# Six of eight output tiles of a 512-token projection as seven-product pairs on one Trainium2 core

## The chip, the cores and the metric

The kernel runs on one core of one Trainium2 chip, in one launch. The metric is the device time of that core in microseconds (us): the median of three runs of the kernel before is 1076.18 us (1074.87 to 1076.5). Differences of a few us, that is of a few tenths of a per cent, are what this case is about. Every number with a row shown beside it comes from one profiled execution, whose instructions are stamped in us from the start of its span.

## The reference, cut to what matters

One decoder layer is applied to 512 prompt tokens and 64 sample tokens (T = 576 columns together). Its first block, the mixer, runs two kinds of heads and joins them by one projection; two further blocks (cross attention to a memory of 256 rows, and a gated feed-forward net) follow.

```python
proj = u @ w_in                                   # u: (tokens, 1024)
...
y_ssd = _rms(...) * g_ssm_out                     # first half of the mixer's output, 1024 wide
h_ml = _rms(h_ml).reshape(bsz, length, ML_INNER) * g_mlstm_out * jax.nn.sigmoid(og)   # second half, 1024 wide
mix = jnp.concatenate([y_ssd, h_ml], axis=-1) @ w_out     # (tokens, 2048) @ (2048, 1024)
x = x + _rms(mix) * g_post_mix
```

The change concerns `y_ssd @ w_out[0:1024]`, the first half of that last product: 1024 x 1024 weights by 1024 x 576 activations.

## The kernel before, in words

**Layout and precision.** Activations lie with features on the 128 partitions and tokens along the free axis, as `[128, 8, 576]` (eight k-tiles of 128 features). Each float32 operand is split into a high part (a rounding cast by ScalarE, `A.copy` into an fp32r tile) and a low part (the rest, subtracted by VectorE); a product is three matmuls per k-tile: high by high, high by low, low by high. An output tile of 128 features thus takes 2 token parts x 8 k-tiles x 3 = 48 matmuls, with the token parts `HALVES` = 256 and 320 columns wide.

**Weights.** `split_w` loads 512 KB into `raw` (two buffers, from the SP queue), casts into `whi` (three buffers, ScalarE, L191) and makes `wlo` (three buffers, VectorE, L198). Where VectorE is spared, the low part is made by a transfer instead: ScalarE writes minus the high part, and a DMA on the POOL queue adds the raw weights from HBM to it.

**The stretch around the change.** The last tiles of the input projection (`in_tile(29 + j, ...)`, "og" tiles; their evacuations are L1133, L1134, L1136) end together with the last mLSTM head, whose normalisation runs on VectorE and GpSimd (`head_norm`, L941 to L954, then L1000) and whose result TensorE transposes (L1004, `ht`, then copied to `qk` at L1005). Between them `gn_apply` (L1122) scales `y` and splits it into `mixs_h` and `mixs_l`. Then come eight calls `out1(j)`: the first half of the output projection, 16 token parts evacuated to `f` by ScalarE (L1154). The first may not go ahead of `ht` on TensorE (`issue_after`). Early in this stretch `mixm_h` and `mixm_l`, the split second half of the mixer's output, are made from `qk` (L1160, L1161), and the samples' part of it from `ogs` (L1165, L1166). Then follow the calls `out2(j, i)`: the second half, added to `f` by VectorE (L1288), with squares and a scaled copy by ScalarE.

**Work placed beside it.** `presplit` takes eight weight matrices of later stages (list `PRE`): load to `prel` (POOL queue), cast (L1244, ScalarE), low part (L1245, VectorE), store to HBM (POOL queue); their casts stand between 403.9 and 442.0 us. `memraw` (the memory, in the slot that held `qk`) is loaded in four pieces during `out1(4)` to `out1(7)`, split by `memory()` (L1274, L1275) and squared; `wm_split` prepares four matrices for the memory's keys and values; `x` takes over that slot afterwards (L1297, two loads) and is first used by `chain2` (L1191).

**Order.** Outside a few stretches written out by hand, a list scheduler decides the order on each engine from a model of the instructions' times: what is ready goes first by place in the program. The order is then fixed; each engine and each queue (SP, POOL) takes its instructions in that order. `tc.issue_after(i)` puts what is in its block behind instruction `i`. Memory of a closed pool is given to the next one; the first write of a new tile waits for the last reader of the old one.

**The same scheme elsewhere.** The feed-forward block already multiplies pairs of output tiles in seven products instead of eight (`Seven`, `Pair`, L1862 to L1998; a Winograd form of the 2 x 2 block product: two feature tiles by two halves of the tokens, two halves of the inner axis). Its token parts are `EHALVES`, 288 columns each, its mixed sums of the activations come from four subtractions (L1825) with casts (L1837) and low parts (L1842), and its mixed sums of the weights are L1898 to L1922.

```python
def mul(s, ps, w, b, start=True):                 # one of the seven products, L1939
    ...
    for k in range(nk):                           # 4 k-tiles
        mm(ps, wh, b[0][k], ...); mm(ps, wh, b[1][k], ...); mm(ps, wl, b[0][k], ...)
```

## Time and profile before

| | |
|---|---|
| three runs | 1074.87, 1076.18, 1076.5 us |
| the profiled execution | 1074.69 us; its span 1072.9 us; granted TensorE clock 0.999 |
| TensorE (PE) busy | 1063.1 us, 99% of the span |
| VectorE (DVE), ScalarE (ACT), GpSimd (POOL) busy | 757.7, 608.9 and 231.0 us |
| moved by DMA | 181.74 MB, 169 GB/s over the span |

How to read it: PE is TensorE's matmuls, PEld its weight loads. A busy share is a share of the time shown, and for PE it says nothing of the rate, so rates are read from the starts of successive matmuls. In a row of a timeline stand the start in us, the duration in us, the engine, the line of the kernel, the operation, output and inputs; in square brackets the idle time ahead of it and what ended it. A row of a line's or tile's listing gives the count and the shortest, median and longest duration in ns. A row of stages gives a stretch, its length, and the busy time of each engine in it (with counts).

### The profile page before, as it was taken

The numbers are of one execution on the slowest core, as the hardware profiler recorded it, in microseconds if no ns is written. First come the engines' busy times: TensorE is split into PE (matmuls) and PEld (weight loads), VectorE is DVE, ScalarE is ACT, GpSimd is POOL, SyncE is SP. The second block draws the span as 40 slices with busy tenths as digits, with TensorE's granted clock in tenths as the row PEclk, the third lists the DMA queues.
The fourth block names the chain that finished last, engine by engine and source line by source line (L and its number), as shares of the span: only waits on it lengthen the run. The fifth ranks groups of instructions, "written<-read, shape, count | busy, mean of one in ns | idle before, by whom it ended". The sixth has DMA issues, their size and how long they took to land.

```text
span 1072.9 us, 20686 instructions
## 1 busy us (share of the span) xinstructions
PE 1063.1 (99%) x8096; PEld 1011.0 (94%) x8096; DVE 757.7 (71%) x1523; ACT 608.9 (57%) x1102; POOL 231.0 (22%) x305
## 2 busy tenths in 40 slices
PE   9999999999999999999999999999999999999997
PEld 8999887778999999999999989999999999999997
DVE  6798775658878774758755556766467887787556
ACT  7778523345654555655555445645566566656654
POOL 0454543313213111000154201100011111111000
PEclk9999999999999999999999999999999999999999
DMA  6776544425655349642468775743476687578532
GB/s 209 176 162 132 158 134 172 147 89 168 196 150 152 106 143 330 235 170 98 158 213 288 265 256 176 254 124 98 133 179 137 160 188 178 114 191 188 144 119 89
DMA packets 58965, 181.74 MB, mean 169 GB/s; under 512 B 6604, under 2 KB 12108, under 8 KB 58356
## 3 DMA queue, kind: packets, MB, share of 16 engines
q1 hardware_dynamic: 42884, 138.22, 38.7%
q0 software_dynamic: 15408, 41.43, 19.7%
q8 instruction: 63, 1.03, 0.4%
q10 hardware_dynamic: 576, 0.79, 0.2%
q14 instruction: 34, 0.28, 0.1%
HBM read 159.75 MB, written 20.65 MB: 168 GB/s over the span
## 4 chain that ended last, share of the span: by engine, by line
PE 98%; DVE 0%; DMA 0%; POOL 0%; issue 0%; ACT 0%; SPq 0%; DVEq 0%
PE ps_in L215 7%; PE ps_in L218 7%; PE ps_in L216 7%; PE ps_v L882 5%; PE ps_g L1946 3%; PE ps_u L1946 3%; PE ps_g L1945 3%; PE ps_o L218 3%; PE ps_o L216 3%; PE ps_u L1947 3%; PE ps_g L1947 3%; PE ps_o L215 3%; PE ps_u L1945 3%; PE ps_dn L1945 2%; PE ps_dn L1947 2%; PE ps_dn L1946 2%
## 5 line engine op out<-in xcount | busy, mean ns | idle before, releaser
L215 PE MATMUL ps_in<-uh,whi 128*128 128x320 f32 (+1 forms) x544 | 162.6, 299 | 0.0
L218 PE MATMUL ps_in<-uh,wlo 128*128 128x320 f32 (+1 forms) x544 | 161.6, 298 | 0.0
L216 PE MATMUL ps_in<-ul,whi 128*128 128x320 f32 (+1 forms) x544 | 161.1, 296 | 0.0
L191 ACT CAST whi<-raw 128x1024 fp32r<-128x1024 f32 (+1 forms) x104 | 105.4, 1015 | 93.3 <-PE ps_in L216 21.5
L198 DVE TENSOR_TENSOR wlo<-raw,whi 128x1024 fp32r<-128x1024 f32 (+2 forms) x97 | 95.3, 983 | 63.7 <-ACT whi L191 63.0
L215 PEld LDWEIGHTS ps_in<-uh,whi 128*128 128x128 f32 x544 | 102.3, 188 | 1.9 <-issue 0.8
L218 PEld LDWEIGHTS ps_in<-uh,wlo 128*128 128x128 f32 x544 | 102.2, 188 | 1.9 <-issue 1.3
L216 PEld LDWEIGHTS ps_in<-ul,whi 128*128 128x128 f32 x544 | 102.4, 188 | 0.5
L196 POOL DMA_DIRECT2D wlo<-win x31 | 27.2, 877 | 80.2 <-ACT wlo L195 69.9
L1945 PE MATMUL ps_g<-b,whi 128*128 128x288 f32 x144 | 42.4, 295 | 0.0
L1946 PE MATMUL ps_g<-b,whi 128*128 128x288 f32 x144 | 42.3, 294 | 0.0
L1946 PE MATMUL ps_u<-b,whi 128*128 128x288 f32 x144 | 42.2, 294 | 0.0
L1945 PE MATMUL ps_u<-b,whi 128*128 128x288 f32 x144 | 42.2, 294 | 0.0
L1905 DVE TENSOR_TENSOR wlo<-sw,whi 128x1024 fp32r<-128x1024 f32 (+1 forms) x26 | 29.6, 1139 | 16.8 <-ACT whi L1904 16.8
L1918 ACT CAST whi<-rawx 128x1024 fp32r<-128x1024 f32 (+1 forms) x26 | 25.6, 986 | 26.2 <-PE ps_dn L1946 13.3
L1895 ACT CAST whi<-raw 128x1024 fp32r<-128x1024 f32 (+1 forms) x26 | 25.6, 985 | 22.8 <-PE ps_g L1946 11.8
L215 PE MATMUL ps_xo<-qh,whi 128*128 128x288 f32 x128 | 38.2, 301 | 0.0
L216 PE MATMUL ps_xo<-ql,whi 128*128 128x288 f32 x128 | 37.8, 297 | 0.0
L218 PE MATMUL ps_o<-mixm_h,wlo 128*128 128x256 f32 (+1 forms) x128 | 37.5, 293 | 0.0
L216 PE MATMUL ps_o<-mixm_l,whi 128*128 128x256 f32 (+1 forms) x128 | 37.5, 293 | 0.0
L218 PE MATMUL ps_xq<-u2h,wlo 128*128 128x320 f32 (+1 forms) x128 | 37.5, 294 | 0.0
L218 PE MATMUL ps_o<-mixs_h,wlo 128*128 128x320 f32 (+1 forms) x128 | 37.4, 293 | 0.0
(788 smaller groups left out, 3855.6 us busy)
## 6 DMA issues: line engine op xcount, KB each, us to landing
raw<-win SPq DMA_DIRECT2D x35, 512.0 KB, 4.4
raw<-wout SPq DMA_DIRECT2D x17, 512.0 KB, 4.2
raw<-wxq SPq DMA_DIRECT2D x13, 512.0 KB, 4.7
raw<-wgate SPq DMA_DIRECT2D x13, 512.0 KB, 3.3
raw<-wup SPq DMA_DIRECT2D x13, 512.0 KB, 4.7
wlo<-win POOLq DMA_DIRECT2D x24, 256.0 KB, 5.6
kva<-vc SPq DMA_DIRECT2D x11, 512.0 KB, 5.9
raw<-wv SPq DMA_DIRECT2D x10, 512.0 KB, 4.0
```

The costliest lines, as they stand in the source:

```text
L191: casts.append(A.copy(hi[:, :n], raw[:, :n]))
L196: accs.append(G.dma_start(lo[:, a:b], src[:, a:b], accum_op=ALU.add))
L198: e.tensor_tensor(lo[:, a:b], raw[:, a:b], hi[:, a:b].bitcast(F32), op=ALU.subtract)
L215: mm(ps, wh, ah, start=i == 0, stop=False)
L216: products.append(mm(ps, wh, al, start=False, stop=False))
L218: m = mm(ps, tiles[order[c]][1], xh(order[c], t0, n), start=False, stop=c == len(tiles) - 1)
L882: mm(ps, a, b, skip_group_check=True, **kw)
L1895: s.c1 = A.copy(s.h1[:, s.all], s.r1[:, s.all])
L1905: V.tensor_tensor(s.l2[:, s.all], sw[:, s.all], s.h2[:, s.all].bitcast(F32), op=ALU.subtract)
L1945: mm(ps, wh, b[0][k], start=start and k == 0, stop=False, skip_group_check=True)
L1946: mm(ps, wh, b[1][k], start=False, stop=False, skip_group_check=True)
L1947: m = mm(ps, wl, b[0][k], start=False, stop=k == nk - 1, skip_group_check=True)
```

## The change

Tiles 0 and 1 of the first half stay as they are. Tiles 2 to 7 become three pairs of a new class `Mixed`, which do what the feed-forward pairs do: seven products of four k-tiles with 288 columns, summed in two places by TensorE in one bank and otherwise by VectorE into `f` (`put`). The activations' four mixed sums are made in place in `y` (`mixed_sums`), with high and low parts in a new pool `mixsums`; the weights' sums use a new pool `mixweights` that takes the memory of the closed mLSTM pools. The first weights' low part comes from VectorE for the first pair and by transfer for the other two. One operand of each pair (`h4`, `ls`) is written over columns of `mixs_h` and `mixs_l` that are no longer read. `ghalf` is kept in place of the parameters `g_ml`; the samples' part of `mixm` is made ahead of `out1(0)`, the rest of `mixm` three, three and two tiles at a time behind each pair's last cast and last low part. One of the eight matrices made ahead (`raw_ahead`, `low_ahead`, `store_ahead`) is done during the pairs, with the low part by transfer; the other seven, and the memory's loads, move behind the pairs into the second half of the projection.

```diff
-    ghalf = ml.tile([P, KT], F32, name="ghalf")
-    V.tensor_scalar(ghalf, PAR("g_ml"), 0.5, None, op0=ALU.mult)
+    ghalf = PAR("g_ml")
+    V.tensor_scalar(ghalf, ghalf, 0.5, None, op0=ALU.mult)
...
+    sos = ExitStack()
+    wo = sos.enter_context(tc.tile_pool(name="mixsums", bufs=1, side="right", reuse_waits="tile"))
+    tmh, tml = [[wo.tile([P, 4, 288], F32R, name=k + str(m), tag=k + str(m)) for m in range(4)] for k in ("tmh", "tml")]
+    ES = [slice(t0, t0 + n) for t0, n in EHALVES]
+    (M11, M12), (M21, M22) = [[y[:, 4 * k:4 * k + 4, c] for c in ES] for k in range(2)]
...
+    def mixed_sums(*ops):
+        for m, o, p, q in ops:
+            V.tensor_tensor(o, p, q, op=ALU.subtract)
+            split(tmh[m], tml[m], o)
...
+    mixed_sums((0, M11, M12, M11), (2, M12, M22, M12), (1, M22, M22, M11), (3, M21, M21, M22))
+
+    def mixm_parts(js, p_):
+        for j in js:
+            hm = qk[:, 4 * (j % 2) + j // 2, 0:TP]
+            with tc.issue_after(p_.cast.ins):
+                A.activation(mixm_h[:, j, 0:TP], hm, AF.Copy, scale=ghalf[:, j:j + 1])
+            with tc.issue_after(p_.low.ins):
+                V.scalar_tensor_tensor(mixm_l[:, j, 0:TP], hm, ghalf[:, j:j + 1], mixm_h[:, j, 0:TP].bitcast(F32),
+                                       op0=ALU.mult, op1=ALU.subtract)
...
+    mixm_samples()
+    stv.close()
+    svs = ExitStack()
+    wv = svs.enter_context(tc.tile_pool(name="mixweights", bufs=1, reuse_waits="tile"))
...
+    HA, HB, HALL = slice(0, 512), slice(512, 1024), slice(0, 1024)
+    m11, m21, m22 = [[[t_[:, 4 * k + m, c] for m in range(4)] for t_ in (mixs_h, mixs_l)]
+                     for k, c in ((0, ES[0]), (1, ES[0]), (1, ES[1]))]
+    tm = [[[t_[m][:, k, :] for k in range(4)] for t_ in (tmh, tml)] for m in range(4)]
...
+    class Mixed:
+        def __init__(s, j):
+            s.j, s.side = j, j // 2 % 2
+            src = [I["wout"][j + k, 0] for k in range(2)]
+            s.r1 = wp.tile([P, 1024], F32, name="raw", tag="raw", bufs=2)
+            s.r2 = wv.tile([P, 1024], F32, name="rawm", tag="rawm", bufs=2)
+            for r, w in zip((s.r1, s.r2), src):
+                loads.append(S.dma_start(r, w))
+            h1, h2, h3 = [wp.tile([P, 1024], F32R, name="whi", tag="whi", bufs=3) for _ in range(3)]
+            l2, l3 = [wp.tile([P, 1024], F32R, name="wlo", tag="wlo", bufs=3) for _ in range(2)]
+            l1 = wv.tile([P, 1024], F32R, name="waccm", tag="waccm", bufs=2)
+            h4, ls = [t_[:, 0:4, 288 + P * s.side:416 + P * s.side] for t_ in (mixs_h, mixs_l)]
+            sm = wv.tile([P, 1024], F32, name="swm", tag="swm")
+            d4 = wv.tile([P, 512], F32, name="d4m", tag="d4m")
+            def low_by_transfer(out, raw, w):
+                A.activation(out, raw, AF.Copy, scale=-1.0)
+                G.dma_start(out, w, accum_op=ALU.add)
+            if j == 2:
+                with tc.issue_after(evs[1].ins):
+                    A.copy(h1, s.r1)
+                V.tensor_tensor(l1, s.r1, h1.bitcast(F32), op=ALU.subtract)
+            else:
+                low_by_transfer(l1, s.r1, src[0])
+                A.copy(h1, s.r1)
+            low_by_transfer(l3[:, HA], s.r2[:, HB], src[1][:, HB])
+            V.tensor_tensor(sm[:, HB], s.r2[:, HA], s.r2[:, HB], op=ALU.add)
+            V.tensor_tensor(sm[:, HA], sm[:, HB], s.r1[:, HA], op=ALU.subtract)
+            split(h2, l2, sm)
+            V.tensor_tensor(s.r2[:, HA], s.r1[:, HA], s.r2[:, HA], op=ALU.subtract)
+            V.tensor_tensor(d4, s.r1[:, HB], sm[:, HA], op=ALU.subtract)
+            A.copy(h3, s.r2)
+            V.tensor_tensor(ls, k4(s.r2[:, HA]), k4(h3[:, HA]).bitcast(F32), op=ALU.subtract)
+            s.cast = A.copy(h4, k4(d4))
+            s.low = V.tensor_tensor(k4(l3[:, HB]), k4(d4), h4.bitcast(F32), op=ALU.subtract)
+            s.w = [(k4(h1[:, HA]), k4(l1[:, HA])), (k4(h1[:, HB]), k4(l1[:, HB])), (k4(h2[:, HA]), k4(l2[:, HA])),
+                   (k4(h2[:, HB]), k4(l2[:, HB])), (k4(h3[:, HA]), ls), (k4(h3[:, HB]), k4(l3[:, HA])), (h4, k4(l3[:, HB]))]
+        def bank(s):
+            return (MP if s.side else GP)("ps_o")[:, :288]
+        def mul(s, ps, w, b, start=True):
+            fh, fl = s.w[w]
+            for k in range(4):
+                mm(ps, fh[:, k, :], b[0][k], start=start and k == 0, stop=False, skip_group_check=True)
+                mm(ps, fh[:, k, :], b[1][k], start=False, stop=False, skip_group_check=True)
+                m = mm(ps, fl[:, k, :], b[0][k], start=False, stop=k == 3, skip_group_check=True)
+            return m
+        def put(s, a, i, ps, first):
+            o = f[:, s.j + a, ES[i]]
+            if first:
+                evs.append(A.copy(o, ps))
+            else:
+                V.tensor_tensor(o, o, ps, op=ALU.add)
+        def early(s):
+            s.x, y_ = s.bank(), s.bank()
+            with tc.issue_after(whole.ins) if s.j == 2 else ExitStack():
+                s.mul(s.x, 0, m11)
+            s.put(0, 0, s.x, True)
+            s.mul(y_, 1, m21)
+            s.put(0, 0, y_, False)
+        def mid(s):
+            s.mul(s.x, 2, tm[1], False)
+            s.put(0, 1, s.x, True)
+            s.z = s.bank()
+            s.mul(s.z, 3, tm[0])
+            s.mul(s.x, 4, tm[2], False)
+            s.put(1, 1, s.x, True)
+            s.put(1, 1, s.z, False)
+        def late(s):
+            s.mul(s.x, 5, tm[3], False)
+            s.put(1, 0, s.x, True)
+            s.mul(s.z, 6, m22, False)
+            s.put(0, 1, s.z, False)
...
+    PRE = [("xo", 0), ("xo", 1), ("g", 0), ("u", 0), ("g", 1), ("u", 1), ("g", 2), ("u", 2)]
+    pre = dr.tile([P, len(PRE), 1024], F32, name="pre")
+    ahead, turns = [], list(range(len(PRE)))
+    def ahead_src(n):
+        k, j = PRE[n]
+        return I[{"xo": "wxo", "g": "wgate", "u": "wup"}[k]][j]
+    def raw_ahead():
+        n_ = turns.pop(0)
+        t_ = wv.tile([P, 1024], F32R, name="prem", tag="prem")
+        G.dma_start(t_, ahead_src(n_))
+        return n_, t_
+    def low_ahead(n_, t_, p_):
+        with tc.issue_after(p_.cast.ins):
+            A.activation(t_, t_.bitcast(F32), AF.Copy, scale=-1.0)
+        G.dma_start(t_, ahead_src(n_), accum_op=ALU.add)
+    def store_ahead(n_, t_, p_):
+        with tc.issue_after(p_.low.ins):
+            S.dma_start(pre[:, n_, :], t_.bitcast(F32))
+    def presplit(n, left):
+        while len(ahead) > left:
+            n_, t_ = ahead.pop(0)
+            h_ = at.tile([P, 1024], F32R, name="preh", tag="prh", bufs=1)
+            with tc.issue_after(evs[-1].ins):
+                A.copy(h_, t_)
+            V.tensor_tensor(t_, t_, h_.bitcast(F32), op=ALU.subtract)
+            G.dma_start(pre[:, n_, :], t_)
+        for _ in range(n):
+            n_ = turns.pop(0)
+            t_ = at.tile([P, 1024], F32, name="prel", tag=("pr", "prl", "mv")[n_ % 3], bufs=1)
+            G.dma_start(t_, ahead_src(n_))
+            ahead.append((n_, t_))
     def out1(j):
         with tc.issue_after(ht.ins) if j == 0 else ExitStack():
-            gemm2([(*split_w(I["wout"][j, 0], cut=1024), KT)], act(mixs_h), act(mixs_l),
-                  lambda t0, n, ps: evs.append(A.copy(f[:, j, t0:t0 + n], ps)), "ps_o1")
+            return gemm2([(*split_w(I["wout"][j, 0], cut=1024), KT)], act(mixs_h), act(mixs_l),
+                         lambda t0, n, ps: evs.append(A.copy(f[:, j, t0:t0 + n], ps)), "ps_o1")
     out1(0)
-    for j in range(8):
-        hm = qk[:, 4 * (j % 2) + j // 2, 0:TP]
-        with tc.issue_after((evs[0] if j > 2 else htc).ins):
-            A.activation(mixm_h[:, j, 0:TP], hm, AF.Copy, scale=ghalf[:, j:j + 1])
-        V.scalar_tensor_tensor(mixm_l[:, j, 0:TP], hm, ghalf[:, j:j + 1], mixm_h[:, j, 0:TP].bitcast(F32),
-                               op0=ALU.mult, op1=ALU.subtract)
-    o4 = ogs.rearrange("p (h d) t -> p h d t", d=2)
-    for d in range(2):
-        V.scalar_tensor_tensor(o4[:, :, d], o4[:, :, d], 1.0, qk[:, 4 * d:4 * d + 4, TP:T], op0=ALU.add, op1=ALU.mult)
-    V.tensor_tensor(ogs, ogs, ghalf.unsqueeze(2).to_broadcast([P, KT, TS]), op=ALU.mult)
-    split(mixm_h[:, :, TP:T], mixm_l[:, :, TP:T], ogs)
-    stv.close()
+    early_low = raw_ahead()
+    whole = out1(1)
+    before = None
+    for j in (2, 4, 6):
+        pair_ = Mixed(j)
+        pair_.early()
+        if before:
+            before.late()
+        pair_.mid()
+        before = pair_
+        if j == 4:
+            low_ahead(*early_low, pair_)
+        elif j == 6:
+            store_ahead(*early_low, pair_)
+        mixm_parts(range(*{2: (0, 3), 4: (3, 6), 6: (6, 8)}[j]), pair_)
+    before.late()
+    svs.close()
+    sos.close()
     phs = ExitStack()
...
-    for j in range(8):
-        if j:
-            out1(j)
-        presplit(min(len(turns), 1 if j else 2))
-        if j > 3:
-            k2 = slice(2 * j - 8, 2 * j - 6)
-            with tc.issue_after(loads[-1].ins):
-                S.dma_start(memraw[:, k2, :], I["memT"][:, k2, :])
+    presplit(2, 0)
+    for j in range(4):
+        k2 = slice(2 * j, 2 * j + 2)
+        with tc.issue_after(loads[-1].ins):
+            S.dma_start(memraw[:, k2, :], I["memT"][:, k2, :])
     def memory(ks):
...
     for j in range(4):
         out2(j, 1)
         out2(j, 0)
-        presplit(0, 0)
+        presplit(min(len(turns), 2 if j else 1), 1 if j < 3 else 0)
         memory(range(2 * j, 2 * j + 2))
         wm_split(j)
     memory_norm()
```

The pool `mixsums` lies on the right side of the core's memory and is closed, like `mixweights`, ahead of the pools of the next block (`rows`, `attn`), which thus take over its memory.

More of the change, by code (lines that the diff above doesn't have):

```diff
@@ new lines, in mixm_samples @@
+    def mixm_samples():
+        o4 = ogs.rearrange("p (h d) t -> p h d t", d=2)
+        for d in range(2):
+            V.scalar_tensor_tensor(o4[:, :, d], o4[:, :, d], 1.0, qk[:, 4 * d:4 * d + 4, TP:T], op0=ALU.add, op1=ALU.mult)
+        V.tensor_tensor(ogs, ogs, ghalf.unsqueeze(2).to_broadcast([P, KT, TS]), op=ALU.mult)
+        split(mixm_h[:, :, TP:T], mixm_l[:, :, TP:T], ogs)
+    mixm_samples()
+    stv.close()
+    svs = ExitStack()
+    wv = svs.enter_context(tc.tile_pool(name="mixweights", bufs=1, reuse_waits="tile"))
@@ L1147, in build, with k4 @@
     f = SL(5, "f_mix")
     evs = []
+    def k4(t_):
+        return t_.rearrange("p (k c) -> p k c", c=P)
+    HA, HB, HALL = slice(0, 512), slice(512, 1024), slice(0, 1024)
[73 more added lines that the diff above has]
+            s.put(0, 1, s.z, False)
```

18 lines of the change are left out of this document (removed).

## The prediction

> **What bounds the kernel now.** I read the page's busy shares and its chain first, then TensorE's waits.
>
> ```profile
> PE 1063.1 (99%) x8096; PEld 1011.0 (94%) x8096; DVE 757.7 (71%) x1523; ACT 608.9 (57%) x1102; POOL 231.0 (22%) x305
> ...
> PE 98%; DVE 0%; DMA 0%; POOL 0%; issue 0%; ACT 0%; SPq 0%; DVEq 0%
> ```
> ```profile
> PE ps_warm L337 <- DVE wz L334: 1.1, 1, 1.1
> PE ps_in L378 <- ACT uh L361: 1.0, 1, 1.0
> PE ps_rb L1693 <- DVE px_r L1686: 0.6, 1, 0.6
> ```
> The chain that ended last is 98% matmuls, and all of TensorE's waits come to 2.7 us, none near the change. So a matmul less is its time saved, and every us by which another engine makes TensorE wait is lost in full. Next come the stretch of the change (all products of `ps_o` from `mixs`, with its first matmul and the first one of the next stretch) and the busy times of the stages around it.
>
> ```profile
> 384.00:433.90 49.90, 49.83 (x384) 49.85 (x385) 0.00 (x0) 5.81 (x15) 1.00 0.76 260
> ```
> ```profile
> 384.07 0.36 PE L215 MATMUL ps_o<-mixs_h,whi 128*128 128x256 f32 x1
> ...
> 433.92 0.30 PE L215 MATMUL ps_o<-mixm_h,whi 128*128 128x320 f32 x1
> ```
> ```profile
> 371.00:384.00 13.00, 13.00 (x102) 12.78 (x102) 10.91 (x29) 4.76 (x9) 2.24 (x3) 1.00 0.23 82
> 384.00:396.50 12.50, 12.50 (x99) 12.50 (x99) 11.28 (x19) 9.41 (x19) 1.08 (x3) 1.00 0.24 69
> 396.50:434.00 37.50, 37.50 (x292) 37.50 (x291) 18.55 (x21) 20.00 (x35) 5.83 (x11) 1.00 0.93 323
> 434.00:485.00 51.00, 51.00 (x397) 50.95 (x395) 33.95 (x60) 31.61 (x53) 3.84 (x7) 1.00 0.54 195
> 485.00:520.00 35.00, 35.00 (x262) 34.78 (x261) 32.06 (x78) 22.83 (x52) 1.86 (x3) 1.00 0.34 105
> ```
> Columns of the stages: stretch, length, busy us of PE, PEld, DVE, ACT, POOL, granted clock, share of DMA, GB/s. TensorE is full everywhere at a clock of 1.00. VectorE is the engine to watch: 22.19 of 25.5 us ahead of and beside the first two tiles, half idle while the other six run, and 32.06 of 35 us behind the whole projection.
>
> **TensorE's part.** From 384.07 to 433.92 there are 384 matmuls in 49.85 us, 129.8 ns each (half of 256, half of 320 columns). The new products have 288 columns, as those of the feed-forward block, read there in a stretch without a wait:
>
> ```profile
> 801.02 0.29 PE L1945 MATMUL ps_u<-b,whi 128*128 128x288 f32 x1
> ...
> 803.52 0.29 PE L1946 MATMUL ps_g<-b,whi 128*128 128x288 f32 x1
> ```
> Nineteen matmuls lie between the two starts: 131.6 ns each, 1.4% more than the present mean. A pair had 2 x 48 = 96 matmuls and gets 7 x 4 x 3 = 84. Tiles 0 and 1 stay: 96 x 129.8 = 12.46 us. Three pairs: 252 x 131.6 = 33.16 us. Together 45.62 us against 49.85: **-4.23 us**, the gain if nothing waits. (The Trainium skill, TensorE: Matmul & The Clock Gate, section Back-to-back issue gap, gives a warm gap of N / 2.4 + 2.5 ns, 122.5 ns for 288 columns. The 131.6 ns here do not agree; by the page's figure the 36 matmuls saved would be an estimated 4.4 us.)
>
> With these rates TensorE would run tiles 0 and 1 to 396.53, pair 2's first two products to 399.69, its next three to 404.43, pair 4's first two to 407.58, pair 2's last two to 410.74, and so on to 429.69. Those are the due times below.
>
> **VectorE's part.** Rows of the same operations and sizes:
>
> ```profile
> L1825 DVE TENSOR_TENSOR f_xo<-f_xo x4: 1353/1358/1359, 709.4 to 713.5; 128x1152 f32<-128x1152 f32 x4
> L1842 DVE TENSOR_TENSOR b<-f_xo,b x4: 1350/1352/1354, 714.8 to 726.8; 128x1152 fp32r<-128x1152 f32 x4
> L1898 DVE TENSOR_TENSOR sw<-rawx x26: 547/683/693, 725.2 to 999.5; 128x512 f32<-128x512 f32 x18, 128x384 f32<-128x384 f32 x8
> L1161 DVE SCALAR_TENSOR_TENSOR mixm_l<-qk,ghalf,mixm_h x8: 743/744/748, 386.8 to 393.1; 128x512 fp32r<-128x512 f32 x8
> L1245 DVE TENSOR_TENSOR prel<-prel,preh x8: 1224/1226/1230, 405.0 to 443.1; 128x1024 f32<-128x1024 f32 x8
> L1275 DVE SCALAR_TENSOR_TENSOR memhl<-memraw,par,memhl x8: 479/484/489, 396.9 to 413.4; 128x256 fp32r<-128x256 f32 x8
> L2044 DVE TENSOR_TENSOR f_ffn<-f_ffn,ps_dn x56: 443/448/456, 831.8 to 973.0; 128x288 f32<-128x288 f32 x56
> L1160 ACT ACTIVATE mixm_h<-qk,ghalf x8: 719/721/737, 385.2 to 390.4; 128x512 fp32r<-128x512 f32 x8
> L1154 ACT COPY f_mix<-ps_o x16: 349/392/426, 387.7 to 434.9; 128x256 f32<-128x256 f32 x8, 128x320 f32<-128x320 f32 x8
> L1274 ACT ACTIVATE memhl<-memraw,par x8: 493/503/513, 396.4 to 412.8; 128x256 fp32r<-128x256 f32 x8
> L1890 ACT ACTIVATE wacc<-raw x26: 834/1053/1064, 716.3 to 994.0; 128x1024 fp32r<-128x1024 f32 x18, 128x768 fp32r<-128x768 f32 x8
> ```
> Up to the first product that needs a mixed sum (pair 2, 399.69; from 371 that leaves 28.7 us) VectorE has 22.19 us of today; less the eight `mixm_l`, which move behind the pairs (8 x 0.744 = 5.95), and less two plain low parts of later tiles (2 x 1.23 = 2.45); plus four subtractions and four low parts of the mixed sums (4 x 1.358 + 4 x 1.352 = 10.84); plus of pair 2 the low part of the first weights, two half sums and the low part of their sum (1.23 + 1.37 + 1.23 = 3.83). That is **28.46 of 28.7 us**; if the fourth mixed sum, not due before 407.58, is left for later, 25.75. So VectorE goes from a cover to a near-bound here. Taking 0 (the fourth sum gives way) and 3.1 us as ends (all four go first, and the 25.5 - 22.19 = 3.3 us that today lie idle for dependencies cannot be used: 28.46 + 3.3 - 28.7), I take 0.4 us, nearer the lower end, since the mixed sums have few dependencies and fill such gaps.
>
> One such gap is in a chain that TensorE is due to meet:
>
> ```profile
> 381.89 0.16 DVE L951 TENSOR_TENSOR hn_a<-hn_y 128x4 f32<-128x4 f32 x1 [0.94 <-POOL hn_y L950]
> ...
> 382.68 1.14 DVE L1000 TENSOR_SCALAR num<-num,hn_a 128x256 f32<-128x256 f32 x4
> 383.14 1.17 PE L1004 MATMUL ps_ht<-c,num 128*128 128x128 f32 x8
> ```
> The last head's norm ends at 382.68, and the transposes run 383.14 to 384.31, right in time and right ahead of the first tile. A subtraction of 1.36 us put into the idle 0.94 us makes this late by 0.42; begun just before its end, by up to 1.36. Behind it wait the copy to `qk`, the last og evacuations, and with them a bank for the first tile's second part. Ends 0 and 1.36; I take 0.4. Both delays overlap in part (TensorE's wait here gives VectorE time), so I sum them to **+0.8 us** and keep 0 to 4.5.
>
> Per later pair (11.05 us of TensorE) VectorE has two half sums, two differences and two half low parts (6 x 0.683), one whole low part (1.23), three sums into `f` (3 x 0.448) and three `mixm_l` (3 x 0.744): 8.9 us, 81%. ScalarE has four whole passes (`h1`, `h2`, `h3` and the negated copy, 4 x 1.053), an estimated 1.1 for two half passes, four evacuations (4 x 0.392) and three `mixm_h` (3 x 0.721): 9.1 us. The feed-forward block holds that with the same three buffers for the weights:
>
> ```profile
> 850.00:900.00 50.00, 50.00 (x381) 50.00 (x381) 39.00 (x73) 32.19 (x50) 8.60 (x10) 1.00 0.79 184
> ```
> 78% there, with no wait of TensorE, so I cost the later pairs at 0; without that cover each us is a us. Bounds -0 and +1 per pair.
>
> **What moves.** `ghalf`, the samples' part and `mixm_h` change place, not amount; nothing needs `mixm` before 429.69. Seven matrices made ahead go behind the pairs, five of them from this stretch to the second half: 5 x 1.23 us on VectorE, 5 x 1.053 on ScalarE, and 5 x 2 POOL transfers of 512 KB. The eight `memhl` (3.9 us VectorE, 8 x 0.503 on ScalarE) follow, since `memraw` takes the slot of `qk`, which the last `mixm` parts read behind pair 6's cast, at about 418. In the second half VectorE then has 33.95 + 6.1 + 3.9 = 44 of 51 us, ScalarE 31.61 + 5.3 + 4 = 41. DMA falls from a share of 0.93 in the first half and rises from 0.54 in the second, to a level at which today's `out1` runs with no wait. The matrix made during the pairs costs ScalarE two passes and POOL three transfers, off the path. Cost 0; bounds in the rivals.
>
> **Sum.** -4.23 + 0.8 = **-3.4 us**. The profiled execution took 1074.69 us, 1.8 over its span and 1.5 below the median; against the median it is 1076.18 - 3.4 = **1072.8 us**. If this case holds: 1071.2 to 1074.0. A change below 0.2% (2.15 us) can hardly be told from none.
>
> **Rivals.**
> *VectorE becomes the bound at pair 2* (no change). The scheduler takes the sums as they stand in the program, all four ahead of pair 2's weights, and their low parts can lie in memory of the mLSTM buffers, free only after 384.3. Then the 3.1 us are paid in full: 1076.18 - 4.23 + 3.1 = 1075.1. For it: 28.46 of 28.7. Against it: TensorE meets no wait today with VectorE at 32.06 of 35 us.
>
> *The memory's chain comes late* (slower).
> ```profile
> 393.90 0.33 SPq L1270 DMA_DIRECT2D memraw<-memT  x1
> ```
> ```profile
> 461.97 0.33 SPq L1297 DMA_DIRECT2D x<-xT  x1
> ```
> ```profile
> 491.90 2.89 DVE L1191 TENSOR_TENSOR x<-x,f_mix 128x320 f32<-128x320 f32 x7
> ```
> ```profile
> x<-xT SPq DMA_DIRECT2D x2, 1152.0 KB, 9.6
> ```
> `x` is loaded into the memory's slot and used 30 us later, 4.2 earlier after the change: 487.7. The load takes 9.6 us, so an issue after 478 delays `chain2`, which VectorE runs at 92% already, and behind it the queries' products. If the whole chain shifts as its first load does (393.9 to about 418), `x` is issued at 486 and lands 8 us late: 1076.18 - 4.23 + 8 = 1080. The gain is gone from an issue at 482 on. Against it: the squares that hold the slot follow their place in the program, and VectorE has 7 us to spare.
>
> *POOL's transfers starve beside a busier VectorE* (slower).
> ```profile
> wacc<-wgate POOLq DMA_DIRECT2D x9, 512.0 KB, 7.2
> ```
> Pair 6's first low part is such a transfer: `raw` is free after pair 2's last difference (about 402.5), load 4, pass 1.05, transfer 7.2, thus 414.8 against a due time of 415.5. Doubled, it is 6.5 us late: 1076.18 - 4.23 + 6.5 = 1078.5. Against it: the same ring at 78% of VectorE makes no wait. [...]
>
> *The change doesn't save the products* (no change): only if TensorE spaced them wider than 131.6 ns; nothing in the rows says so.
>
> **Chances.** Forecast 0.61; VectorE the bound, or products not saved, 0.22 (0.20 and 0.02); the memory's chain 0.12; POOL's transfers 0.05. Thus faster 0.61, same 0.22, slower 0.17. The range goes from 1071.0 (no wait at all, less a us of spread) to 1077.6, leaving out the worst of the slower cases.
>
> **What the next profile shows.** Right: 96 + 252 products of `ps_o` from `mixs`, `out2` starting 3 to 4.2 us earlier, TensorE's waits under 1.5 us between 383 and 430. Wrong: a wait at the transposes, at pair 2's third product on VectorE, or on `ql`, `u2l` or `x` after 485; 288-column products apart by more than 132 ns; or equal time of this stretch given back behind 434.

## The result and the profile after

The changed kernel takes 1086.11 us (median of 6 runs, 1085.03 to 1089.2), the kernel before beside it 1076.09 us (6 runs). The ratio is 1.0097, with a 95% interval of 1.0087 to 1.0108: **10 us slower**, where 3.4 us faster was forecast. The profiled execution took 1087.15 us, its span is 1085.4 us. Read first, as before the change, the busy shares and the chain that ended last, then TensorE's waits.

```profile
PE 1064.1 (98%) x8060; PEld 1010.7 (93%) x8060; DVE 776.3 (72%) x1555; ACT 619.7 (57%) x1117; POOL 238.9 (22%) x310
...
PE 82%; issue 8%; DMA 5%; POOL 2%; DVE 1%; ACT 1%; SPq 0%; DVEq 0%; POOLq 0%; ACTq 0%
```
```profile
PE ps_ss L249 <- DVE ssqo L303: 6.6, 1, 6.6
PE ps_ht L1004 <- DVE num L1000: 2.5, 1, 2.5
PE ps_in L215 <- DVE tmp L1143: 1.4, 1, 1.4
...
PE ps_o L1237 <- DVE wlo L203: 0.8, 1, 0.8
```
The matmuls are fewer by the 36 that the change was to save (8096 to 8060), but the chain is no longer 98% TensorE. Four new waits, 11.3 us together, all stand between 380 and 487 us. The stages of this stretch (columns as in the prediction: stretch, length, busy us of PE, PEld, DVE, ACT, POOL, clock, share of DMA, GB/s):

```profile
371.00:384.00 13.00, 11.63 (x90) 11.43 (x89) 12.96 (x22) 3.64 (x8) 2.74 (x2) 1.00 0.25 81
384.00:396.50 12.50, 9.95 (x69) 9.69 (x68) 9.34 (x21) 6.07 (x9) 2.52 (x3) 0.86 0.24 85
396.50:434.00 37.50, 36.55 (x274) 36.08 (x273) 27.99 (x44) 27.13 (x43) 5.82 (x8) 1.00 0.75 182
434.00:485.00 51.00, 46.06 (x349) 45.86 (x347) 33.33 (x55) 31.61 (x56) 6.91 (x15) 0.97 0.86 310
485.00:520.00 35.00, 33.27 (x243) 32.76 (x244) 28.86 (x68) 22.01 (x45) 4.18 (x6) 0.89 0.30 107
```
Neither VectorE nor ScalarE is at its limit behind 384, and yet TensorE stands. The first product of the queries, the first work behind the whole stretch, starts 12.2 us later: in the kernel before

```profile
496.72 0.45 PE L215 MATMUL ps_xq<-u2h,whi 128*128 128x320 f32 x2
```
and in the changed one

```profile
508.95 0.45 PE L215 MATMUL ps_xq<-u2h,whi 128*128 128x320 f32 x2
```
Behind this point the distance stays: the first `ps_xo` product comes at 629.0 instead of 616.5, 12.5 us late, and the span is longer by 12.5 us. So the loss lies ahead of 509, in two places. (The two profiled executions differ by 12.5 us and the medians by 10.0: the one before (1074.69 us) is faster than all six runs beside it, the changed one the second slowest of its six. The prices read from rows below are those of the profiled executions.)

**First loss: around 384.** VectorE's own rows, in its order:

```profile
375.84 1.36 DVE L1132 TENSOR_TENSOR xs<-xs 128x1152 f32<-128x1152 f32 x1
377.11 0.22 DVE L941 SCALAR_TENSOR_TENSOR hn_d<-num 128x4 f32<-128x4 f32 x1
...
379.06 1.35 DVE L1132 TENSOR_TENSOR xs<-xs 128x1152 f32<-128x1152 f32 x1
380.33 0.16 DVE L942 TENSOR_TENSOR hn_d<-hn_d,expnm 128x4 f32<-128x4 f32 x1
...
381.13 1.35 DVE L1132 TENSOR_TENSOR xs<-xs 128x1152 f32<-128x1152 f32 x1
382.40 0.17 DVE L943 RECIPROCAL hn_d<-hn_d 128x4 f32<-128x4 f32 x1
...
382.95 1.35 DVE L1132 TENSOR_TENSOR xs<-xs 128x1152 f32<-128x1152 f32 x1
384.22 0.15 DVE L947 TENSOR_TENSOR hn_v<-hn_d 128x4 f32<-128x4 f32 x1
...
386.78 1.14 DVE L1000 TENSOR_SCALAR num<-num,hn_a 128x256 f32<-128x256 f32 x4
```
Each of the four subtractions (L1132) stands right ahead of one small step of the last head's norm. The norm is a chain of steps of 0.2 us; until 384.22 it now takes one step per subtraction, and the scaling (L1000) begins at 386.78 instead of 382.68. An evacuation of the last og tiles (`tmp`, L1143), behind the second subtraction, is late as well: that is the 1.4 us wait. TensorE's rows behind the norm:

```profile
387.19 1.97 PE L1004 MATMUL ps_ht<-c,num 128*128 128x128 f32 x8 [2.55 <-DVE num L1000]
388.81 0.56 PE L215 MATMUL ps_o<-mixs_h,whi 128*128 128x256 f32 x1
...
389.60 0.41 PE L215 MATMUL ps_o<-mixs_h,whi 128*128 128x256 f32 x1
...
390.13 0.28 PE L215 MATMUL ps_o<-mixs_h,whi 128*128 128x256 f32 x1
```
Tile 0 starts at 388.81, 4.74 us late, and its first five products are 0.20 to 0.36 us apart, not 0.117: another 0.6 us.

**Second loss: 474 to 492.** Four views of one chain, in order of cause: POOL's queue, ScalarE, VectorE, TensorE.

```profile
465.01 0.54 POOL L1301 DMA_DIRECT2D pre<-prel  x1
...
472.73 0.53 POOL L1305 DMA_DIRECT2D prel<-wgate  x1 [5.58 <-DMA pre<-prel]
```
```profile
482.19 1.04 ACT L1299 CAST preh<-prel 128x1024 fp32r<-128x1024 f32 x1 [7.46 <-DMA prel<-wgate]
```
```profile
474.58 0.48 DVE L303 TENSOR_TENSOR ssqo<-ssqo,sq 128x320 f32<-128x320 f32 x1
483.26 1.23 DVE L1300 TENSOR_TENSOR prel<-prel,preh 128x1024 f32<-128x1024 f32 x1 [8.20 <-ACT preh L1299]
484.40 0.49 DVE L303 TENSOR_TENSOR ssqo<-ssqo,sq 128x320 f32<-128x320 f32 x1
```
```profile
486.70 0.90 PE L249 MATMUL ps_ss<-c,ssqo 128*128 128x128 f32 x3 [6.64 <-DVE ssqo L303]
...
488.68 0.41 PE L216 MATMUL ps_o<-mixm_l,whi 128*128 128x256 f32 x1
488.90 0.41 PE L218 MATMUL ps_o<-mixm_h,wlo 128*128 128x256 f32 x1
```
A matrix made ahead is loaded at 472.73, when the store that held its buffer has landed; the load itself takes 9.4 us. ScalarE's cast of it and VectorE's low part are already next in their queues and stand still for 7.46 and 8.20 us. Behind them on VectorE stand a sum of squares of `out2`'s results, whose squares were ready at 474.3, and an addition to `f` whose products were done as well; TensorE waits 6.64 us for what comes of them. Then its products of 256 columns start 0.213 us apart until 492, almost twice the 0.113 of the stretch ahead of the wait: some 2.4 us more.

**The sum of the changed kernel**, from the starts of its matmuls: products -4.08 (the 288-column ones are 132.2 ns apart where nothing waits, not 131.6, which gave -4.23); around 384 +5.65 (the wait on `tmp` with its slow restart 1.64, the transposes 2.7 + 0.7, tile 0's slow start 0.6); pair 2 +1.5 (the 0.84 us wait on its second weights, and slow spacing around it); the wait at `ps_ss` +6.8 and the slow products behind it +2.35: **+12.2 us**, against +12.2 to 12.5 in the trace.

### The profile page after: what moved, and what is told of

Same layout as the page of the kernel before. It is cut to its first block, busy times and chain, and to the rows that moved or that the text cites. A ratio compares the mean times of both kernels' runs of the same rounds, so it can differ in the third digit from the quotient of the medians.

```text
span 1085.4 us, 20685 instructions
## 1 busy us (share of the span) xinstructions
PE 1064.1 (98%) x8060; PEld 1010.7 (93%) x8060; DVE 776.3 (72%) x1555; ACT 619.7 (57%) x1117; POOL 238.9 (22%) x310
## 4 chain that ended last, share of the span: by engine, by line
PE 82%; issue 8%; DMA 5%; POOL 2%; DVE 1%; ACT 1%; SPq 0%; DVEq 0%; POOLq 0%; ACTq 0%
PE ps_in L215 6%; PE ps_in L218 6%; PE ps_in L216 6%; PE ps_v L882 5%; PE ps_g L2082 3%; PE ps_u L2082 3%; PE ps_g L2081 3%; PE ps_u L2083 3%; PE ps_g L2083 3%; PE ps_u L2081 3%; PE ps_dn L2081 2%; PE ps_dn L2083 2%; PE ps_dn L2082 2%; PE ps_dn L215 2%; PE ps_dn L218 2%
## 5 line engine op out<-in xcount | busy, mean ns | idle before, releaser
L191 ACT CAST whi<-raw 128x1024 fp32r<-128x1024 f32 (+1 forms) x98 | 99.0, 1012 | 86.4 <-PE ps_in L216 18.4
L198 DVE TENSOR_TENSOR wlo<-raw,whi 128x512 fp32r<-128x512 f32 (+2 forms) x91 | 87.8, 966 | 52.4 <-ACT whi L191 51.0
L215 PE MATMUL ps_o<-mixm_h,whi 128*128 128x256 f32 (+1 forms) x128 | 38.6, 302 | 0.0
L2031 ACT CAST whi<-raw 128x1024 fp32r<-128x1024 f32 (+1 forms) x26 | 25.6, 985 | 22.0 <-PE ps_g L2082 11.8
L215 PE MATMUL ps_xq<-u2h,whi 128*128 128x320 f32 (+1 forms) x128 | 37.5, 295 | 0.0
```

What stands on the lines that cost most here:

```text
L191: casts.append(A.copy(hi[:, :n], raw[:, :n]))
L198: e.tensor_tensor(lo[:, a:b], raw[:, a:b], hi[:, a:b].bitcast(F32), op=ALU.subtract)
L215: mm(ps, wh, ah, start=i == 0, stop=False)
L2031: s.c1 = A.copy(s.h1[:, s.all], s.r1[:, s.all])
```

## Experiments

The theory from here on is *order*: each engine works its queue in order (as above, where squares that are ready stand behind a cast that waits), and the loss is short, urgent work queued behind long or late work that nobody waits for. The rivals are *amount* (VectorE, ScalarE or the DMA carry too much there, and no order helps), and, for the second loss, the memory's parts, which moved as well. In the diffs, "changed" is the kernel after the change. Differences are medians against the kernel before in the same series of runs (1074.9 to 1075.7 us); the changed kernel stands at +10.0.

**1. Subtractions behind the norm** (on the changed kernel):
```
-            V.tensor_scalar(num[:, c, 0:256], ...)
+            scaled = V.tensor_scalar(num[:, c, 0:256], ...)
...
-    mixed_sums(...)
+    with tc.issue_after(scaled.ins):
+        mixed_sums(...)
```


> The changed kernel, with the four subtractions of the mixed sums held until the last head's numerators are scaled (L1000); nothing else differs. Theory (order on VectorE): in the changed kernel these four, 1.35 us each, stand between the small steps of the head's norm, which so ends at 386.78 instead of 382.68; with them behind it the transposes run near 383.1 again, the 2.55 us wait and the 1.37 us wait on the tmp tile go, and the time falls by 4 to 6 us, to 1080 to 1082. The 6.6 us wait at ps_ss near 486 stays. Rival (amount of VectorE's work): the 10.8 us of sums have to be done ahead of pair 2 in any order, so the wait only moves, to the first evacuations into f_mix (which wait for the low parts of the sums) or to pair 2's third product, and the time stays at 1084 to 1087.

Measured 1090.69 us, **+15.3** (ratio 1.0139, 1.0118 to 1.0160): slower still. The waits at the transposes and on `tmp` are gone, as the theory said, but TensorE and ScalarE show a new one:

```profile
PE ps_o L215 <- ACT f_mix L1313: 3.8, 1, 3.8
```
```profile
397.36 0.98 ACT L1313 COPY f_mix<-ps_o 128x256 f32<-128x256 f32 x3 [0.65 <-DVE tml L203]
```
`f_mix` has the slot of the tile that holds the sums (`xs`), so its first evacuation waits for the last low part of all four sums, and both banks of the first tiles stay full until then. In the changed kernel that was hidden: the evacuation ran at 396.40, and tile 0 was late by as much. The theory had missed a second chain; the rival had named this wait, though the time is over its range too. In the profiles this run is 1.6 us slower than the changed kernel (the wait at `ps_ss` is 7.8 us here), in the medians 5.3; that difference is not explained.

**2. Five matrices made ahead, not eight:**
```
-    PRE = [("xo", 0), ("xo", 1), ("g", 0), ("u", 0), ("g", 1), ("u", 1), ("g", 2), ("u", 2)]
+    PRE = [("xo", 0), ("xo", 1), ("g", 0), ("u", 0), ("g", 1)]
```


> The changed kernel, with five matrices made ahead instead of eight (the last three get their low parts in the feed-forward block as the later ones do). Theory (one late load blocks queues that run in order): the load of the last-but-one matrix, issued at 472.73 after a store had landed, lands at 482.2; ScalarE's cast and VectorE's low part stand and wait for it, and behind them the squares that ps_ss needs. With five there is no such load behind 465, the wait of 6.6 us at ps_ss goes and the slower matmuls after it, and the time falls by 6 to 9 us to 1077 to 1080; the wait at the transposes stays. Rival (total load behind 434: DMA at a share of 0.86, VectorE and ScalarE two thirds busy): 3 of 7 matrices less takes away some load, but the memory's eight parts remain late, and a wait of 3 us or more stays at ps_ss: 1082 to 1085. Second rival: the work left out comes back as waits in the feed-forward block, time 1083 to 1086.

Measured 1080.96 us, **+5.6** (1.0046, 1.0029 to 1.0063). The wait at `ps_ss` is gone and TensorE is full from 434 to 520; the queries start at 500.7. The time is 1 us over the theory's range: some 2.5 us come back in the feed-forward block, as the second rival said, in waits longer than the 0.6 us that both kernels have there:

```profile
PE ps_rb L1829 <- DVE px_r L1822: 1.5, 2, 0.9
...
PE ps_rb L1829 <- DVE p_r L1822: 0.8, 1, 0.8
```

**3. Both edits 1 and 2.** 

> Both edits: subtractions held behind the head's norm, and five matrices made ahead. Theory: both losses go, the 36 products saved remain: 1071.5 to 1074, 2 to 4.5 under the kernel before. Rival (amount of work): 1079 to 1085, with waits at pair 2 or at ps_ss.

Measured 1081.16 us, **+5.8** (1.0048, 1.0033 to 1.0064): the theory's number missed by 7 us, since edit 1 only moves its wait to `f_mix` (3.8 us again).

**4. The kernel before, with seven of the matrices moved and nothing else changed:**
```
-        presplit(min(len(turns), 1 if j else 2))
+        if j < 2:
+            presplit(1 - j, 0 if j else 1)
...
+    with tc.issue_after(evs[-1].ins):
+        presplit(2, 0)
...
-        presplit(0, 0)
+        presplit(min(len(turns), 2 if j else 1), 1 if j < 3 else 0)
```


> The kernel before, all its products as they were, with only seven of the eight matrices made ahead moved behind the first half, with the changed kernel's order of loads, casts and stores there; the memory's parts stay where they were. Theory: the late load blocks here too, and the time rises by 4 to 9 us to 1080 to 1085, with the wait at ps_ss on the squares. Rival (it is the memory's parts or the sum of all that moved, not the matrices): no wait, 1075.5 to 1077.5.

Measured 1082.46 us, **+7.1** (1.0057, 1.0041 to 1.0073). The same block without a pair, a mixed sum or a moved memory part. The time is in the theory's range, but what TensorE waits for is not the squares at `ps_ss`: it is the memory's norm (`rmem_r`), which stands behind the same low part on VectorE and which TensorE meets first here. ScalarE and TensorE of this run:

```profile
474.16 1.04 ACT L1244 CAST preh<-prel 128x1024 fp32r<-128x1024 f32 x1 [7.30 <-DMA prel<-wgate]
```
```profile
478.93 0.66 PE L287 MATMUL ps_rb<-c,rmem_r 128*128 128x128 f32 x2 [5.28 <-DVE rmem_r L276]
```

**5. As 4, the last two matrices finished later:**
```
-        presplit(min(len(turns), 2 if j else 1), 1 if j < 3 else 0)
+        presplit(min(len(turns), 2 if j else 1), 1 if j < 3 else 2)
...
     with tc.issue_after(m.ins):
         rstd_rows(rc, HCHUNKS[1], rb, B0)
+        presplit(0, 0)
```


> The kernel before with seven matrices made ahead moved behind the first half, as in the run where only these were moved, but the last two finished behind the products of out2's tile 6. Theory: the 5.3 us wait of that run goes, and the time is that of the kernel before: 1075 to 1077. Rival (it is the moved load as such): 1080 to 1083.

Measured 1076.15 us, **+1.3** (1.0008, 0.9999 to 1.0018). All seven matrices are made, all their transfers run, VectorE's and ScalarE's work is the same; only the place in the queue of two casts and two low parts (and so the time of their stores) differs. That takes back 6 of the 7 us, so the loss of run 4 is order, not amount.

**6. The changed kernel with edit 5.** 

> The changed kernel with all eight matrices made ahead, but the casts and low parts of the last two issued behind the last products of out2's tile 6, that is behind the squares and the norm that TensorE waits for; their loads start where they did. Theory (a late load blocks queues that run in order): the 6.6 us wait at ps_ss goes without any work being left out, and nothing is paid in the feed-forward block: 1077 to 1079.5. Rival (total load of DMA and engines behind 434): the wait stays or moves to the chain of norms behind 485: 1083 to 1087.

Measured 1079.86 us, **+5.0** (1.0046, 1.0031 to 1.0061). No wait at `ps_ss`, no payment in the feed-forward block. So the same edit takes back 5 of the changed kernel's 10 us; the theory had 0.4 us more. (In this run's profile, the fastest of its four executions, the queries start at 499.9, 3.2 us late, close to the 3.1 of the sum above without the second loss; the median lies 1.3 us over the profiled time.) With the memory's parts as late as in the changed kernel, and a DMA share of 0.88 from 434 to 485, the highest of these runs in that stretch, TensorE does not wait there:

```profile
434.00:485.00 51.00, 51.00 (x393) 50.99 (x392) 38.99 (x69) 36.34 (x65) 8.23 (x16) 1.00 0.88 324
```

**7. The kernel before, with the four subtractions and no other part of the change:**
```
...
+    for o, p, q in ((M11, M12, M11), (M12, M22, M12), (M22, M22, M11), (M21, M21, M22)):
+        V.tensor_tensor(o, p, q, op=ALU.subtract)
```


> The kernel before, with only the four subtractions added (in place, on data no longer used; no low parts, no pairs): 5.4 us of VectorE. Theory (order): they stand among the small steps of the last head's norm as in the changed kernel, the norm ends some 4 us late, TensorE waits about 2.5 us at the transposes and 1 to 1.4 us on the tmp tile: 1078 to 1081. Rival (amount): VectorE is idle for 3.3 of the 25.5 us there and TensorE meets nothing: 1074.5 to 1076.5.

Measured 1080.96 us, **+5.3** (1.0051, 1.0038 to 1.0065). 5.4 us of VectorE, on an engine that is not full, cost 5.3 us of time, by the two waits of the changed kernel:

```profile
PE ps_ht L1004 <- DVE num L1000: 2.6, 1, 2.6
PE ps_in L215 <- DVE tmp L1133: 1.4, 1, 1.4
```

**8. Edit 1, and `f` written into the very tile of the sums**, so that an evacuation waits only for the low parts that read its own rows:
```
-    f = SL(5, "f_mix")
+    f = y
```


> The changed kernel with the subtractions held behind the last head's norm, and f_mix written into the very tile that held the sums' sources (f = y), so that an evacuation waits only for the low parts of its own rows, not for all four. Theory (the loss between 380 and 402 is order on VectorE, and behind it the shared slot of f_mix): no TensorE wait at the transposes and none of the 3.8 us at the first evacuations; pair 2 starts near 396.5 to 397.5; the wait at ps_ss behind 474 stays: 1080 to 1083, 3 to 6 less than the changed kernel. Rival (amount of VectorE's work ahead of pair 2): the wait moves once more, to pair 2's third product on its weights, and nothing is gained: 1085 to 1089.

Measured 1083.92 us, **+9.0** (1.0085, 1.0069 to 1.0100). The waits at the transposes, on `tmp` and on `f_mix` are gone or down to 0.2 us, but two are left at pair 2 (and one of 0.6 us at pair 4):

```profile
PE ps_o L1238 <- DVE wlo L203: 1.4, 1, 1.4
...
PE ps_o L1238 <- DVE waccm L1213: 0.9, 1, 0.9
```
Pair 2 begins near 396.5, and VectorE is busy for 12.50 of the 12.5 us ahead of it. Here both theories are half right: a part of the loss was order, and a part moves on to the next due time. The 6.3 us wait at `ps_ss` is still in this run.

**9. Edits 5 and 8 together.** 

> Both: subtractions held and f in place, the last two matrices made ahead finished behind the norm. Theory: the 36 products saved are left as a gain: 1071 to 1073.5, 2.5 to 5 under the kernel before. Rival: 1076 to 1083 with a new wait at pair 2 or behind 485.

Measured 1077.21 us, **+2.3** (1.0025, 1.0014 to 1.0036): within the rival's range, with the 0.9 and 1.4 us at pair 2 and a wait of 1.5 us on `u2l`, in the stretch into which two low parts had been moved.

**10. As 9, the fourth sum behind pair 2's second weights:**
```
-    ... (1, M22, M22, M11), (3, M21, M21, M22))
+    ... (1, M22, M22, M11))
...
         pair_ = Mixed(j)
+        if j == 2:
+            with tc.issue_after(pair_.low2.ins):
+                mixed_sums((3, M21, M21, M22))
```


> As the run with both edits, and the fourth sum (M21), which no product needs before pair 2's last two, is subtracted and split behind the low part of pair 2's second weights: 2.7 us of VectorE less ahead of that low part. Theory (what is left at pair 2 is amount of work with a due time): the waits there, 0.9 and 1.4 us, fall to under 0.8 together, and the time falls by 1.5 to 2.5 us to 1074.5 to 1075.8; the 1.5 us wait on u2l behind 485 stays. Rival (the weights come late from their loads or from ScalarE's order): the waits stay, 1076.5 to 1078.

(`low2` is the low part of the second weights.) Measured 1077.12 us, **+1.4** (1.0019, 1.0007 to 1.0030), which can't be told from run 9: the theory's time was missed. The wait on `waccm` is gone, that on the second weights is not (1.4 us), and a second one of 0.8 us stands at pair 4. The wait on `u2l`, which was expected to stay, is not in this profile. ScalarE's and VectorE's rows tell why:

```profile
400.16 0.40 ACT L1245 COPY xs<-ps_o 128x288 f32<-128x288 f32 x1 [0.89 <-PE ps_o L1239]
400.45 1.05 ACT L1220 CAST whi<-swm 128x1024 fp32r<-128x1024 f32 x1
```
```profile
401.55 0.46 DVE L1247 TENSOR_TENSOR xs<-xs,ps_o 128x288 f32<-128x288 f32 x1 [1.73 <-ACT whi L1220]
401.93 0.68 DVE L1223 TENSOR_TENSOR d4m<-raw,swm 128x512 f32<-128x512 f32 x1
402.53 1.22 DVE L1221 TENSOR_TENSOR wlo<-swm,whi 128x1024 fp32r<-128x1024 f32 x1
```
The sum to be cast (`swm`) is ready at 399.2. Its cast stands behind an evacuation that waits for TensorE, and the low part behind a sum and a difference that nobody waits for: 1.2 us and 1.0 us. VectorE is idle meanwhile, so this is order.

**11. As 10, and the last two matrices finished still later**, behind the query projection's tile 4:
```
     m = xq(4, 1)
     with tc.issue_after(m.ins):
         rc2[1] = rstd_cols([ssq2], HCHUNKS[1], "p21", alloc=B1)
+        presplit(0, 0)
```


> As the run before it in this list, and the last two matrices made ahead are finished behind the query projection's tile 4 instead of behind out2's tile 6, out of the stretch in which VectorE forms the queries' inputs. Theory: the wait on u2l goes as well, 1.5 to 2.2 us: 1072.5 to 1074.3, which is the kernel before less 1 to 2.5. Rival: the wait comes back further on, or the matrices' stores delay the attention's tiles: 1075 to 1077.

Measured 1078.27 us, **+2.6** (1.0026, 1.0014 to 1.0037): the theory failed. The wait on `u2l` that it was to remove was already absent in run 10. The two low parts ran at 496.09 and 501.71, in the middle of the stretch they were to leave, and TensorE waited three times there:

```profile
PE ps_ss L241 <- DVE ssqo L303: 1.5, 1, 1.5
...
PE ps_xq L215 <- DVE mko L1503: 1.2, 1, 1.2
PE ps_xq L215 <- ACT qsm L1539: 1.1, 1, 1.1
```
The first of these waits ends at 495.09, ahead of both low parts, so they did not make it. The likely cause is another late load at the head of two queues: ScalarE's cast `whi` at 487.37 had stood 6.17 us for its weights (`raw<-wxq`), and VectorE behind it 5.8 us. What made the other two was not tried.

**12. As 9, with the order at pair 2 set by hand** (no work taken away):
```
-            split(h2, l2, sm)
+            s.c2 = A.copy(h2, sm)
+            s.low2 = V.tensor_tensor(l2, sm, h2.bitcast(F32), op=ALU.subtract)
...
+            with tc.issue_after(s.c2.ins) if s.j == 2 else ExitStack():
                 s.put(0, 0, s.x, True)
             s.mul(y_, 1, m21)
+            with tc.issue_after(s.low2.ins) if s.j == 2 else ExitStack():
                 s.put(0, 0, y_, False)
```
and the two differences of pair 2 behind `low2` in the same way. 

> As the run with both edits, all four sums ahead as there, but at pair 2 the order of the small steps is set by hand: ScalarE's cast of the second weights goes ahead of the evacuation that waits for TensorE's first product, and VectorE's low part of them goes ahead of the sum into f and of the two differences. No work is taken away. Theory (what is left at pair 2 is again order, a short step with a due time behind steps without one): the 1.45 us wait on wlo falls below 0.5, the 0.9 us on waccm stays: 1075 to 1076.5. Rival (amount of VectorE's work ahead of pair 2): the wait stays, 1076.5 to 1078.

Measured 1077.86 us, **+2.9** (1.0030, 1.0016 to 1.0044). The wait on the second weights falls from 1.45 to 0.2 us, as the theory said, and the time does not: two waits on evacuations appear behind it, 2.5 us together.

```profile
PE ps_o L1241 <- ACT xs L1249: 2.5, 2, 1.4
```
The time is the rival's. So at pair 2 order alone moves the wait on to the next due time, which speaks for too much work ahead of it, by about as much; run 13 tests that.

**13. Edits 10 and 12 together**, with the fourth sum's cast ahead of the `mixm_h` on ScalarE ("the gates' parts" below). 

> As the run before it in this list, with the fourth sum behind the low part of pair 2's second weights, and its cast ahead of the gates' parts on ScalarE. Theory (order and amount together): no wait of TensorE between 384 and 434 but 0.2 to 0.5 us, out2 starts 3 to 4 us earlier than in the kernel before, and the time is 1072.5 to 1074.5, the first that is under the kernel before. Rival (the gain is eaten further on, where VectorE forms the queries' inputs): 1075 to 1077.

Measured 1073.24 us (11 runs, 1072.56 to 1075.25) against 1075.01 us: **-1.8 us, ratio 0.9983 (0.9975 to 0.9992)**, the one version that is faster than the kernel before, by an interval that just leaves out 1. The time is the theory's, though one wait is longer than it had. Of its waits only two lie in the stretch of the change:

```profile
PE ps_o L1242 <- ACT whi L1221: 1.1, 1, 1.1
...
PE ps_o L215 <- DVE tmp L1144: 0.2, 1, 0.2
```
From the first `ps_o` product to the first `ps_xq` product this run takes 110.5 us, the kernel before 112.6 us. The saved products give 4.1; the wait at pair 4 (on the cast `whi`, with the slower starts around it) takes 1.45, that on `tmp` 0.5 in the same way.

## Why the prediction was wrong

**TensorE's part held.** 36 matmuls are gone, and where nothing waits the new ones start 132.2 ns apart (the mean of 248 of the 252), against the 131.6 read in the feed-forward block; that is over the 132 named as a sign of error, but worth only 0.15 us. The sum of run 13 comes out with 4.1 us for them. The Trainium skill's warm gap (TensorE: Matmul & The Clock Gate, section Back-to-back issue gap, an estimated 122.5 ns for 288 columns), which is given there for an isolated matmul, is not met by these either.

**The step that failed first is the head's norm, costed at 0.4 us with an upper end of 1.36.** The place was right, and so was what waits behind it; the size was not. The prediction put *one* subtraction into the *one* gap that the old trace showed idle. But a chain of small dependent steps can give way at every step: each of four steps found a subtraction begun just ahead of it. The norm's delay is 4.1 us; with the wait on `tmp` and the slow restarts the cost is 5.65 in the changed kernel and 5.3 in run 7, where these subtractions are all that is added. The upper end should have been four times 1.36 = 5.4, one subtraction for each of four steps, and that was to be seen from the rows at hand: the norm has over ten steps between 376.18 and 382.68, and the data of the four subtractions are ready by then.

**VectorE's load ahead of pair 2, costed at 0.4 us with ends of 0 and 3.1.** In the changed kernel 1.5 us, while the late start of tile 0 gave VectorE 4.7 us more; without that cover (run 8) the two waits at pair 2 come to 2.3, and their slow restarts to about another us. So the upper end was the right value once tile 0 starts on time. The reason for the lower one, that the fourth sum gives way, was wrong: the sums ran as they stood in the program, as the rival had it, and only run 13, which makes the fourth give way by hand, comes near the forecast. The shared slot of `f_mix` and the sums, behind which run 1 waited 3.8 us, was in no step of the prediction at all.

**"What moves" was costed at 0, and cost 9 us in the profiled execution (5 us by the medians of run 6).** By the profile its error is the largest of the sum, and it is of kind, not of size. (The norm's cost alone would have turned the gain into a loss too.) It compared sums of busy time (44 of 51 us on VectorE) with the length of the stage. In the trace VectorE is busy for only 33.33 of those 51 us, and TensorE loses 6.6 us all the same, since what blocks is not work but a load that is not there yet, at the head of two queues. The prediction had the numbers: each moved matrix is a chain of load, cast, low part and store, with three buffers and one POOL queue in which a store that lands late holds up the next load. In the kernel before, the last of them began at 442.0 on ScalarE, 29 and 35 us ahead of the two norms that TensorE meets at 471.22 (the memory's) and 477.19. Moved by 46 to 49 us (in the changed kernel its casts run from 449.7 to 491.4, not from 403.9 to 442.0), the chain runs into both. Runs 4 and 5 show it alone: 7.1 us, and 1.3 with two of the seven put behind the norms.

**Rivals.** *VectorE the bound at pair 2* was there, in run 8 at its full price, but as the smaller part. *The memory's chain* did not decide: `x` was issued at 472.29, ahead of the 478 named, and in run 6, with the memory's parts where the change put them, TensorE is full from 434 to 485.

```profile
472.29 0.33 SPq L1433 DMA_DIRECT2D x<-xT  x1
```
*POOL's transfers starving* did not happen at pair 6, where the prediction looked; their landing times did decide, at another place. Besides the spacing, three of the signs of error that the prediction named did show: a wait at the transposes, one at pair 2's third product, and time given back behind 434. What was missing was a rival in which matrices and norm meet in one queue.

## What to carry to other kernels

A sum of busy times says whether an engine can do the work, not whether it does it in time: for every instruction that a change adds or moves, ask what stands behind it in its queue and when the data ahead of it land. A chain of many short steps on a busy engine can lose one long instruction per step, so its bound is the number of steps (or of long instructions) times their length, not one gap. When a wait is taken away, look at once for the next due time, and judge an edit by the time of the whole; here the waits around 384, at pair 2 and at `ps_ss` had to go together before the saved products showed.

## What the runs showed of the hardware

Behind a wait TensorE can restart slowly, and for a time that varies. In the changed kernel the granted clock falls to 0.86 in the stage of the 2.55 us wait and to 0.89 in the one that follows the start of the 6.64 us wait; products of 256 columns then start 213 ns apart, 19 of them in a row after the long wait (488.47 to 492.31), five after the short one. The 213 ns are what the Trainium skill, TensorE: Matmul & The Clock Gate, section Back-to-back issue gap, gives for half the clock (N / 1.2, an estimated 213 for 256 columns). The Trainium skill, TensorE: Matmul & The Clock Gate, section What's actually happening, puts the loss of clock behind an idle window of about 3.4 us; here shorter waits (2.55 us, and 1.45 us in run 11) do it too, and not each time. The wait of 1.45 us at pair 2 stands in runs 9, 10 and 11; in the profiles of 9 and 10 the products behind it are at full rate at once, in that of 11 they are at full rate for 0.8 us and then 240 ns apart for 3.1 us (403.34 to 406.46), which shows in the clock of 0.95:

```profile
396.50:434.00 37.50, 35.74 (x253) 35.04 (x252) 27.89 (x42) 25.17 (x39) 6.05 (x10) 0.95 0.77 193
```
That may be why the versions with waits of about 1.4 us scatter (1076.49 to 1083.77 us in run 12, whose profile shows no slow products) while run 13, with a longest wait of 1.1 us in this stretch, lies within 2.7 us; this was not tried by itself.
